# Pairs 0 and 1 projected among the seven value products, value weights summed in SBUF by accumulating DMAs, x mixed on VectorE

## The chip, the cores and the metric

The kernel runs on one core of one Trainium2 chip, in float32. The metric is device time in microseconds (us). TensorE (PE) multiplies; VectorE (DVE), ScalarE (ACT) and GpSimd (POOL) work on tiles; SP and POOL issue DMAs. A profile of one execution has the start and duration of each instruction, what released it, the DMA packets and the clock that TensorE was granted.

## What is computed

A trunk of two layers over 512 tokens of 1024 numbers: neighbourhood attention in layer 0, latent attention in layer 1, each with a SiLU gate, and a gated embedding behind each. The change is in layer 0, whose mixer is, cut short:

```python
def mixer_na(xn, w_in, rpb, w_out):
    q, k, v, z = jnp.split(xn @ w_in, 4, axis=-1)      # 1024 columns each, 16 heads of 64
    o = neighbourhood_attention(q, k, v, rpb)          # softmax over a window of keys
    return (o * jax.nn.silu(z)) @ w_out
```

`xn` is the input behind a root mean square norm. Queries, keys, gates and values are four products of `xn` with 1024 x 1024 weights.

## The kernel before, in words

**Split numbers.** A float32 operand is split into hi (rounded, a copy on ACT) and lo, the rest (operand minus hi, a subtraction on DVE or POOL). A product is hi·hi + lo·hi + hi·lo, three matmuls where there was one. So every weight piece of 128 x 1024 costs, ahead of its matmuls, a DMA into `wraw` (or `v`), an ACT copy (`whi`) and a DVE or POOL subtraction (`wlo`). Of `wraw`, `whi` and `wlo` there are three buffers each in the shared pool (`wp`).

**Gates first.** `run` (L1016) turns x into columns: `xT` holds normed x in two tiles of 4 x 512; copies `xh` (L1076, ACT) and rests `xl` (L1077, DVE and POOL in turn) are the right sides. In the meantime `z_phase` (L164) projects five gates (`z`), whose matmuls end the first part of TensorE's work.

**Values in seven products.** The value projection is a 2 x 2 block product computed with seven block products in place of eight (Strassen's scheme). The blocks are halves of x (tokens by halves of the 1024 numbers) and quarters of the weights. Products 7, 5, 6 and 3 need mixed x: four sums or differences of halves of `xT` on POOL (L1084), their copies `V7`, `V5`, `V6`, `V3` on ACT (L1087) and rests on DVE (L1088). Products 7, 6, 4 and 5 need mixed weights: `values_seven` (L224) loads four quarters in eight tiles `v` (L232), and DVE adds them in place (L246); copies (L251) are ACT's, rests (L253) DVE's and POOL's. The products go 1, 2, 7, 6, 4, 5, 3 (L283), 24 matmuls of 128 x 512 each, in six PSUM banks: 2 is summed into 1's banks, 4 into 7's, 5 and 3 into 6's. Between products DVE and ACT add and subtract banks (L268, L287 to L296) and split the results into the value tiles `Q` (L94, L96).

**Attention.** `na_heads` (L309) then runs over eight pairs of heads. `project(j)` (L314) loads the two weight pieces of the pair's queries and keys, multiplies them (two products of 24 matmuls, L107) and splits the results into `sa`, `sb` and `da`, `db` (halves by ACT copies), with rests on DVE. `attend(j)` (L347) runs the pair's two heads: scores (L404, L405), bias and row maxima on DVE, exponentials on ACT, the normalisation on POOL, transposes (L439, L441) and the product with the values (L453). The projections of pair j+1 go ahead of the attention of pair j. Between heads POOL issues DMAs (`sum_step`, L571) that sum the quarters of a later weight in DRAM; these are plain (bypass) or accumulating (add).

**What sets the order.** Each engine runs its own instructions in a fixed order, which a scheduler chose when the program was built; `issue_after` in the code ties one instruction behind another. A tile that reuses the memory of an older one waits for that one's readers.

Of the kernel before, what the change touches and what calls it, by code (L numbers as in the profile page):

```python
# [40 lines left out]
class Trunk:  # L41
# [182 lines left out]
    def values_seven(self, pool, xT, X, Q):  # L224

        nc = self.nc
        R = {p: [pool.tile([P, 1024], F32, name=f"v{p}{c}", bufs=1) for c in range(2)] for p in (1, 2, 3, 5)}
        src = {1: (0, 0), 2: (0, 2), 5: (1, 0), 3: (1, 2)}
        for p in (1, 2, 5, 3):
            for c in range(2):  # L230
                n, c0 = src[p]
                nc.sync.dma_start(R[p][c], self.a["na_v"][n, c0 + c])  # L232
        home = {7: (5, 5, 3, ALU.add), 6: (5, 5, 1, ALU.add), 4: (2, 2, 5, ALU.add), 5: (1, 5, 3, ALU.subtract)}
        order = (1, 2, 7, 6, 4, 5, 3)
        W, C, s1, s17, s6 = {}, {}, {}, {}, {}
        pieces = 0

        def prep(p):
            nonlocal pieces
            W[p] = []  # L240
            for c in range(2):
                raw = R[p][c] if p not in home else None
                if raw is None:
                    d, x, y, op = home[p]
                    raw = R[d][c]
                    nc.vector.tensor_tensor(out=raw, in0=R[x][c], in1=R[y][c], op=op)  # L246
                own = pieces < 5 or pieces % 5 < 3
                pieces += 1
                hi, lo = ((self.wp if own else pool).tile([P, 1024], F32R, name=t, tag=t if own else "vw", bufs=3 if own else 4)
                          for t in ("whi", "wlo"))  # L250
                nc.scalar.activation(hi, raw, AF.Copy)  # L251
                for o in (slice(0, S), slice(S, 2 * S)):
                    (nc.gpsimd if c else nc.vector).tensor_tensor(out=lo[:, o], in0=raw[:, o], in1=hi[:, o].bitcast(F32),  # L253
                                                                  op=ALU.subtract)
                W[p].append((hi, lo))

        def left(p, s, k, i):
            if p in X:
                return X[p][:, 2 * s + k // 2, k % 2 * 256 + i * P:k % 2 * 256 + (i + 1) * P]
            half, t = {1: (0, i), 2: (1, i), 4: (1, 2 + i)}[p]  # L260
            return xT[s][half][:, k, t * P:(t + 1) * P]

        def out(th, n, i, ps):
            self.v_split(Q[th, n][:, 2 * i:2 * i + 2, :], ps)

        banks = {1: "mm", 7: "S", 6: "T"}
        base = {2: 1, 4: 7, 5: 6, 3: 6}
        sub = lambda o, x, y: nc.vector.tensor_tensor(out=o, in0=x, in1=y, op=ALU.subtract)  # L268
        for p in order[:2]:
            prep(p)  # L270
        mm = self.last_mm
        for n, p in enumerate(order):
            if n + 2 < len(order):
                prep(order[n + 2])
            for i in range(2):
                if p in banks:
                    C[p, i] = self.psum(banks[p])
                ps = C[base.get(p, p), i]
                m = [(left(p, s, k, i), W[p][k // 2][r][:, k % 2 * S:(k % 2 + 1) * S])
                     for c in range(2) for s, r in ((0, 0), (1, 0), (0, 1)) for k in (2 * c, 2 * c + 1)]  # L280
                for j, (l, r) in enumerate(m):
                    with self.tc.issue_after(mm.ins):
                        mm = nc.tensor.matmul(ps, l, r, start=j == 0 and p in banks, stop=j == 11 and p in (2, 3, 4),  # L283
                                              skip_group_check=True)
                if p == 1:
                    s1[i] = self.temp("s1")
                    nc.scalar.activation(s1[i], ps, AF.Copy)  # L287
                elif p == 2:
                    out(0, 0, i, ps)
                elif p == 7:  # L290
                    nc.vector.tensor_tensor(out=ps, in0=ps, in1=s1[i], op=ALU.add)
                    s17[i] = pool.tile([P, S], F32, name="s17", tag="s", bufs=4)
                    nc.scalar.activation(s17[i], ps, AF.Copy)
                elif p == 6:
                    s6[i] = pool.tile([P, S], F32, name="s6", tag="s", bufs=4)
                    nc.scalar.activation(s6[i], ps, AF.Copy)  # L296
                    sub(C[7, i], C[7, i], s6[i])
                elif p == 4:
                    out(1, 0, i, ps)
                elif p == 5:  # L300
                    q = self.psum("O" if i else "T")
                    sub(q, ps, s17[i])
                    sub(ps, ps, s1[i])
                    out(1, 1, i, q)
                else:
                    out(0, 1, i, ps)
        self.last_mm = mm

    def na_heads(self, pool, xT, zs, oT, Q):  # L309
# [1019 lines left out]
```

## Time and profile before

| what | us |
|---|---|
| three runs | 674.4, 675.49, 675.76; median 675.49 |
| the profiled execution | 673.86 |
| its span, first to last instruction | 671.8 |
| PE busy | 644.6 |
| DVE, ACT, POOL busy | 436.5, 453.0, 448.4 |
| mean granted clock of PE | 0.983 |

A row of a group of instructions has line, engine, operation, out<-in by the program's names, shapes and the count, then the busy time. A row of a timeline starts with the start and duration in us; the time in brackets is the engine's idle time ahead of it and who ended it. A wait of PE costs time, since PE is busy 96% of the span; the others' waits cost only where PE waits for them.

### The profile page before, as it was taken

The numbers are of one execution on the slowest core, as the hardware profiler recorded it, in microseconds if no ns is written. First come the engines' busy times: TensorE is split into PE (matmuls) and PEld (weight loads), VectorE is DVE, ScalarE is ACT, GpSimd is POOL, SyncE is SP. The second block draws the span as 40 slices with busy tenths as digits, with TensorE's granted clock in tenths as the row PEclk, the third lists the DMA queues.
The fourth block names the chain that finished last, engine by engine and source line by source line (L and its number), as shares of the span: only waits on it lengthen the run. The fifth ranks groups of instructions, "written<-read, shape, count | busy, mean of one in ns | idle before, by whom it ended". The sixth has DMA issues, their size and how long they took to land.

```text
span 671.8 us, 9959 instructions
## 1 busy us (share of the span) xinstructions
PE 644.6 (96%) x3299; PEld 543.7 (81%) x3299; DVE 436.5 (65%) x880; ACT 453.0 (67%) x887; POOL 448.4 (67%) x393
## 2 busy tenths in 40 slices
PE   9965899999999999999999999999999999999994
PEld 6854678888888888888899888888888888888884
DVE  6278963557686752567861723688889886474675
ACT  7564454878787764388764544787988898536855
POOL 0496556659797865389844743685978978436974
PEclk9996999999999999999999999999999999999998
DMA  9880004549796999645644425320121213494524
GB/s 325 335 311 3 0 1 160 178 149 224 193 252 184 234 218 250 248 158 186 193 150 130 137 71 146 98 67 10 56 63 59 69 48 125 176 334 134 163 89 157
DMA packets 44755, 102.17 MB, mean 152 GB/s; under 512 B 4640, under 2 KB 17696, under 8 KB 44704
## 3 DMA queue, kind: packets, MB, share of 16 engines
q1 hardware_dynamic: 33776, 83.97, 37.1%
q0 software_dynamic: 10496, 16.78, 11.6%
q10 hardware_dynamic: 432, 0.79, 0.3%
q8 instruction: 26, 0.43, 0.3%
q14 instruction: 25, 0.20, 0.1%
HBM read 89.99 MB, written 25.17 MB: 171 GB/s over the span
## 4 chain that ended last, share of the span: by engine, by line
PE 90%; POOL 3%; DVE 2%; ACT 2%; issue 1%; DMA 1%; POOLq 0%; ACTq 0%; DVEq 0%
PE ps_mm L107 30%; PE ps_S L107 11%; PE ps_mm L804 6%; PE ps_T L139 6%; PE ps_T L696 5%; PE ps_O L916 4%; PE ps_mm L696 3%; PE ps_S L696 3%; PE ps_T L107 2%; PE ps_T L283 2%; PE ps_O L453 2%; PE ps_O L107 2%; PE ps_mm L754 2%; POOL xT L1084 2%; PE ps_mm L184 2%; PE ps_T L441 2%
## 5 line engine op out<-in xcount | busy, mean ns | idle before, releaser
L84 POOL TENSOR_TENSOR wwlo<-wraw,wwhi 128x1024 fp32r<-128x1024 f32 (+5 forms) x70 | 123.7, 1779 | 59.0 <-ACT wwhi L83 46.8
L641 POOL TENSOR_TENSOR wlo<-wraw,whi 128x512 fp32r<-128x512 f32 x56 | 72.6, 1335 | 23.3 <-ACT whi L639 21.2
L83 ACT ACTIVATE wwhi<-wraw 128x1024 fp32r<-128x1024 f32 (+5 forms) x73 | 57.2, 807 | 40.3 <-PE ps_mm L107 14.3
L901 POOL TENSOR_TENSOR ex<-ex,rc 128x512 f32<-128x512 f32 x64 | 66.1, 1041 | 26.5 <-DVE rc L900 22.4
L899 ACT ACTIVATE ex<-ps_S,mx 128x512 f32<-128x512 f32 x64 | 44.0, 687 | 12.1 <-DVE mx L897 10.5
L897 DVE TENSOR_REDUCE mx<-ps_S 128x1 f32<-128x512 f32 x64 | 43.7, 683 | 8.5 <-PE ps_S L107 7.6
L96 DVE TENSOR_TENSOR pt_lo<-ps_T,pt_hi 128x512 fp32r<-128x512 f32 x64 | 43.1, 681 | 7.1 <-ACT pt_hi L94 6.7
L427 POOL TENSOR_TENSOR ex<-ex,rc 128x128 f32<-128x128 f32 (+1 forms) x64 | 36.5, 640 | 14.3 <-DVE rc L423 13.5
L107 PE MATMUL ps_mm<-xh,wwhi 128*128 128x512 f32 x152 | 42.1, 403 | 0.0
L94 ACT ACTIVATE pt_hi<-ps_T 128x512 fp32r<-128x512 f32 x64 | 37.7, 595 | 3.3 <-PE ps_T L139 3.0
L107 PE MATMUL ps_mm<-xl,wwhi 128*128 128x512 f32 x152 | 40.0, 396 | 0.0
L107 PE MATMUL ps_mm<-xh,wwlo 128*128 128x512 f32 x152 | 39.3, 393 | 0.0
L139 PE MATMUL ps_T<-ident,ex 128*128 128x128 f32 x256 | 38.3, 272 | 0.0
L139 PEld LDWEIGHTS ps_T<-ident,ex 128*128 128x128 f32 x256 | 31.5, 140 | 7.5
L421 ACT ACTIVATE ex<-ex,mx 128x128 f32<-128x128 f32 (+1 forms) x64 | 30.3, 474 | 6.9 <-DVE mx L411 4.0
L253 POOL TENSOR_TENSOR wlo<-v,whi 128x512 fp32r<-128x512 f32 x14 | 22.7, 1647 | 17.6 <-ACT whi L251 17.5
L107 PEld LDWEIGHTS ps_mm<-xl,wwhi 128*128 128x128 f32 x152 | 28.0, 188 | 5.6
L107 PEld LDWEIGHTS ps_mm<-xh,wwlo 128*128 128x128 f32 x152 | 28.0, 188 | 5.6
L209 POOL TENSOR_TENSOR u<-u,z 128x512 f32<-128x512 f32 x16 | 21.5, 1345 | 16.2 <-DVE u L205 10.4
L639 ACT ACTIVATE whi<-wraw 128x1024 fp32r<-128x1024 f32 x28 | 29.3, 1057 | 3.4 <-DMA wraw<-sum 2.4
L107 PEld LDWEIGHTS ps_mm<-xh,wwhi 128*128 128x128 f32 x152 | 27.1, 189 | 4.6
L205 DVE TENSOR_TENSOR u<-ps_O,u 64x512 f32<-64x512 f32 x32 | 21.9, 684 | 12.7 <-ACT u L204 12.3
(465 smaller groups left out, 1936.6 us busy)
## 6 DMA issues: line engine op xcount, KB each, us to landing
sum<-gate POOLq DMA_DIRECT2D x12, 1024.0 KB, 8.2
wraw<-na_qk SPq DMA_DIRECT2D x16, 512.0 KB, 3.6
wraw<-sum SPq DMA_DIRECT2D x16, 512.0 KB, 3.3
pe<-pe SPq DMA_DIRECT2D x31, 256.0 KB, 6.3
wraw<-gate SPq DMA_DIRECT2D x12, 512.0 KB, 3.4
v<-na_v SPq DMA_DIRECT2D x8, 512.0 KB, 6.7
sum<-sum POOLq DMA_DIRECT2D x4, 1024.0 KB, 11.9
wraw<-na_o SPq DMA_DIRECT2D x8, 512.0 KB, 4.4
```

What stands on the lines that cost most here:

```text
L83: nc.scalar.activation(hi[:, c], raw[:, c], AF.Copy)
L84: f = lambda e, c=c: e.tensor_tensor(out=lo[:, c], in0=raw[:, c], in1=hi[:, c].bitcast(F32), op=ALU.subtract)
L94: self.last_copy = nc.scalar.activation(hi, src, AF.Copy, scale=scale)
L96: nc.vector.tensor_tensor(out=lo, in0=src, in1=hi.bitcast(F32), op=ALU.subtract)
L107: last = self.last_mm = nc.tensor.matmul(out, l, r, start=i == 0, stop=i == n - 1)
L139: self.last_mm = self.nc.tensor.transpose(t[:, i * P:(i + 1) * P], b, self.ident)
L641: nc.gpsimd.tensor_tensor(out=lo[:, o], in0=raw[:, o], in1=hi[:, o].bitcast(F32), op=ALU.subtract)
L696: mm = nc.tensor.matmul(ps, l, r, start=j == 0 and p in banks, stop=j == 11 and p in (2, 3, 4), skip_group_check=True)
L804: self.last_mm = nc.tensor.matmul(PS[key], *terms[i], start=i == 0, stop=i == len(terms) - 1)
L897: nc.vector.reduce_max(mx, sp, axis=AX.X, negate=True)
L899: nc.scalar.activation(ex, sp, AF.Exp, bias=mx, accum_out=sm)
L901: nc.gpsimd.tensor_tensor(out=ex, in0=ex, in1=rc.to_broadcast([P, S]), op=ALU.mult)
```

## The change

Three things move.

1. `na_heads` is entered before the values. Its `project` is cut into parts: `load(j)` (the weights), `product`, `queries` and `keys`. Pair 0 is projected ahead of value product 1, and pair 1 between products 2 and 7, through `early` (L338 is their matmul in the new numbering; L277 is that of the value products). Pair 0's weights and the first value piece are loaded and split while x is still being prepared. The attention's tiles `ex`, `pt` and so on are in a pool of their own (`nah`) that opens behind the values.
2. The value weights are no longer loaded as four quarters and added by DVE. Unmixed quarters are loaded piece by piece into `wraw`. The mixed ones come from two tiles of 1 MB: `T1` is loaded, and three accumulating DMAs, issued by POOL, add quarters to it one after another; its state after each is the weight of products 7, 6 and 4. `T2` is loaded and added to once (product 5). The rests of all value weights are DVE's. The banks of products 1 and 6 change (`S` and `mm` in place of `mm` and `T`).
3. The four mixes of x (L1137 now) are DVE's, no longer POOL's, and of the rests of x DVE makes the first four and POOL the last four, where they took turns.

```diff
+    def raw_piece(self, n, c, after=None):
+        raw = self.wp.tile([P, 1024], F32, name="wraw", tag="wraw", bufs=3)
+        with self.tc.issue_after(after.ins) if after else nullcontext():
+            self.nc.sync.dma_start(raw, self.a["na_v"][n, c])
+        return raw
+    def values_seven(self, pool, xT, X, Q, piece, project):
+        quarter = lambda n, c: self.a["na_v"][n, c:c + 2].rearrange("c p n -> p c n")
+        T = pool.tile([P, 2, 1024], F32, name="T1", bufs=1)
+        first = nc.sync.dma_start(T, quarter(1, 0))
+        T2 = pool.tile([P, 2, 1024], F32, name="T2", bufs=1)
+        add = lambda t, n, c: nc.gpsimd.dma_start(t, quarter(n, c), accum_op=ALU.add, max_dma_last_dim=4096)
+        add(T, 1, 2)
...
+        project(0)
+        W[1].append(made(self.raw_piece(0, 1, first), False))
+        W[2] = [made(self.raw_piece(0, 2 + c), True) for c in range(2)]
+        product(1)
+        project(1, True)
+        W[7] = [made(T[:, c, :], c) for c in range(2)]
+        product(2)
+        add(T, 0, 0)
+        project(1, False)
+        W[6] = [made(T[:, c, :], True) for c in range(2)]
+        product(7)
+        add(T, 0, 2)
+        nc.sync.dma_start(T2, quarter(1, 0))
+        add(T2, 0, 0)
+        W[4] = [made(T[:, c, :], False) for c in range(2)]
+        product(6)
+        W[5] = [made(T2[:, c, :], True) for c in range(2)]
+        product(4)
+        W[3] = [made(self.raw_piece(1, 2 + c), not c) for c in range(2)]
+        product(5)
+        product(3)
...
-                (nc.vector, nc.gpsimd)[k % 2].tensor_tensor(out=lo, in0=xs[k], in1=hi.bitcast(F32), op=ALU.subtract)
+                (nc.vector, nc.gpsimd)[k // 4].tensor_tensor(out=lo, in0=xs[k], in1=hi.bitcast(F32), op=ALU.subtract)
...
+            weights = {0: [self.load_w(a["na_qk"][i], 1024) for i in (0, 8)]}
+            piece = self.piece(None, self.raw_piece(0, 0), True)
...
-                nc.gpsimd.tensor_tensor(out=d, in0=d, in1=y, op=op)
+                nc.vector.tensor_tensor(out=d, in0=d, in1=y, op=op)
```

`made` is `piece`: an ACT copy and two half rests on DVE.

**The order on ACT.** Between the copies of mixed x (V) and those of the value weights (whi). Before, from the last gate on:

```order
L177 ACTIVATE z_487<-z_487 128x512
L1087 ACTIVATE V7_491<-xT_164 128x1024
L1087 ACTIVATE V5_495<-xT_164 128x1024
L1087 ACTIVATE V6_499<-xT_165 128x1024
L1087 ACTIVATE V3_503<-xT_165 128x1024
L251 ACTIVATE whi_533<-v10_517 128x1024
```

Now, over the same stretch (whi_504 is the first piece of product 1, whi_622 the second; sa to db are pair 0's queries and keys):

```order
L229 ACTIVATE whi_504<-wraw_502 128x1024
L177 ACTIVATE z_453<-z_453 128x512
L1140 ACTIVATE V7_510<-xT_164 128x1024
L177 ACTIVATE z_487<-z_487 128x512
L1140 ACTIVATE V5_514<-xT_164 128x1024
L1140 ACTIVATE V6_518<-xT_165 128x1024
L1140 ACTIVATE V3_522<-xT_165 128x1024
L344 ACTIVATE sa_577<-ps_mm_552 64x512
L345 ACTIVATE sb_578<-ps_mm_552 64x512
L362 ACTIVATE da_612<-ps_mm_587 64x512
...
L365 ACTIVATE db_613<-ps_mm_587 64x512
L229 ACTIVATE whi_622<-wraw_620 128x1024
```

The first value piece now stands ahead of all mixed x; the second stands behind the evacuation of pair 0's keys.

**The order on POOL.** From the gates' weights (wwlo_424, wwlo_458) to the values. Before:

```order
L84 TENSOR_TENSOR wwlo_424<-wraw_422,wwhi_423 128x1024
L84 TENSOR_TENSOR wwlo_458<-wraw_456,wwhi_457 128x1024
L1077 TENSOR_TENSOR xl0_156<-xT_164,xh0_154 128x512 x2
L1077 TENSOR_TENSOR xl1_157<-xT_165,xh1_155 128x512 x2
L1084 TENSOR_TENSOR xT_164<-xT_164 128x4x256
L1084 TENSOR_TENSOR xT_164<-xT_164,xT_165 128x4x256
L1084 TENSOR_TENSOR xT_165<-xT_165,xT_164 128x4x256
L1084 TENSOR_TENSOR xT_165<-xT_165 128x4x256
L253 TENSOR_TENSOR wlo_539<-v11_518,whi_538 128x512 x2
```

Now (wwlo_492 and wwlo_498 are pair 0's weights, wwlo_673 and wwlo_679 pair 1's; the DMAs are the adds):

```order
L84 TENSOR_TENSOR wwlo_424<-wraw_422,wwhi_423 128x1024
L84 TENSOR_TENSOR wwlo_458<-wraw_456,wwhi_457 128x1024
L84 TENSOR_TENSOR wwlo_492<-wraw_490,wwhi_491 128x1024
L1128 TENSOR_TENSOR xl1_157<-xT_165,xh1_155 128x512 x3
L84 TENSOR_TENSOR wwlo_498<-wraw_496,wwhi_497 128x1024
L1128 TENSOR_TENSOR xl1_157<-xT_165,xh1_155 128x512
...
L248 DMA T1_547<-na_v 128x2x1024
L248 DMA T2_550<-na_v 128x2x1024
L84 TENSOR_TENSOR wwlo_673<-wraw_671,wwhi_672 128x1024
L84 TENSOR_TENSOR wwlo_679<-wraw_677,wwhi_678 128x1024
L248 DMA T1_547<-na_v 128x2x1024 x2
L84 TENSOR_TENSOR wwlo_1125<-wraw_1123,wwhi_1124 128x1024
```

The mixes are gone; one rest of x stands behind wwlo_498; the second and third add to T1 stand behind pair 1's weights, with nothing between them.

**The order on TensorE.** From the last gate's product (ps_mm_462) on. Before, the value products come next:

```order
L107 MATMUL ps_mm_462<-rh0_150,wwlo_458 128x512 x4
L107 MATMUL ps_mm_462<-rh1_151,wwlo_458 128x512 x4
L283 MATMUL ps_mm_565<-whi_533,xh0_154 128x512 x2
L283 MATMUL ps_mm_565<-whi_533,xl0_156 128x512 x2
L283 MATMUL ps_mm_565<-wlo_534,xh0_154 128x512 x2
```

Now pair 0's queries (ps_mm_552) and keys (ps_mm_587) come first:

```order
L107 MATMUL ps_mm_462<-rh1_151,wwlo_458 128x512 x4
L338 MATMUL ps_mm_552<-xh0_154,wwhi_491 128x512 x4
L338 MATMUL ps_mm_552<-xh1_155,wwhi_491 128x512 x4
L338 MATMUL ps_mm_552<-xl0_156,wwhi_491 128x512 x4
L338 MATMUL ps_mm_552<-xl1_157,wwhi_491 128x512 x4
L338 MATMUL ps_mm_552<-xh0_154,wwlo_492 128x512 x4
...
L338 MATMUL ps_mm_587<-xh1_155,wwlo_498 128x512 x4
L277 MATMUL ps_S_641<-whi_504,xh0_154 128x512 x2
```

The 48 matmuls of pair 0 stand between the gates and the values; the last rest of x (xl1_157) is needed by the sixteenth of them.

More of the change, by code (lines that the diff above doesn't have):

```diff
@@ L221, in v_split, with piece @@
         self.split(hi, lo, src)
-    def values_seven(self, pool, xT, X, Q):
+    def piece(self, pool, raw, own):
         nc = self.nc
[L227 to L255, printed above, removed]
@@ new lines, in piece @@
+        hi, lo = ((self.wp if own else pool).tile([P, 1024], F32R, name=t, tag=t if own else "vw", bufs=3 if own else 4)
+                  for t in ("whi", "wlo"))
+        nc.scalar.activation(hi, raw, AF.Copy)
+        for o in (slice(0, S), slice(S, 2 * S)):
+            nc.vector.tensor_tensor(out=lo[:, o], in0=raw[:, o], in1=hi[:, o].bitcast(F32), op=ALU.subtract)
+        return hi, lo
+    def raw_piece(self, n, c, after=None):
[3 more added lines that the diff above has]
+        return raw
```

159 lines of the change are left out of this document (93 added, 66 removed).

## Prediction

> **What bounds the kernel now.** I read the page first, then the waits of TensorE, then its timeline and granted clock round the longest wait. The page:
>
> ```profile
> PE 644.6 (96%) x3299; PEld 543.7 (81%) x3299; DVE 436.5 (65%) x880; ACT 453.0 (67%) x887; POOL 448.4 (67%) x393
> PE   9965899999999999999999999999999999999994
> ```
>
> TensorE is the bound; one slice in 40 is 16.8 us, and the only holes ahead of the last slice are in slices 3 to 5. The waits of TensorE, longest first (who waits, for whom, total, times, longest):
>
> ```profile
> PE ps_mm L283 <- ACT whi L251: 13.5, 1, 13.5
> PE ps_T L283 <- POOL wlo L253: 1.9, 2, 1.7
> PE ps_S L283 <- DVE ps_S L268: 0.8, 2, 0.4
> PE ps_T L283 <- ACT whi L251: 0.6, 1, 0.6
> PE ps_S L283 <- POOL wlo L253: 0.5, 1, 0.5
> ```
>
> All are the value products: 17.3 us. TensorE's timeline gives the stretch to compare:
>
> ```profile
> 42.49 1.97 PE L107 MATMUL ps_mm<-rh,wwlo 128*128 128x512 f32 x8
> 57.98 1.22 PE L283 MATMUL ps_mm<-whi,xh 128*128 128x512 f32 x2 [13.51 <-ACT whi L251]
> 62.21 0.63 PE L283 MATMUL ps_mm<-wlo,xh 128*128 128x512 f32 x2
> 110.49 1.98 PE L107 MATMUL ps_mm<-xh,wwhi 128*128 128x512 f32 x8
> 115.93 1.98 PE L107 MATMUL ps_mm<-xh,wwhi 128*128 128x512 f32 x8
> 127.79 0.28 PE L404 MATMUL ps_S<-db,s 128*128 128x256 f32 x1
> ```
>
> From 110.49 to 115.93 are 24 matmuls: 0.227 us each. The gates' last matmul ends at 44.46. Up to 127.79 come seven products of 24, four projections of 24 (pairs 0 and 1) and the 8 short score matmuls of head 0: 264 x 0.227 + 1.0 = 60.9 us of work in 83.3 us. So 22.4 us are lost there. What the waits don't hold is mostly the clock:
>
> ```profile
> 60.00:62.00 2.00, 2.00 (x7) 1.55 (x6) 2.00 (x2) 0.00 (x0) 2.00 (x2) 0.51 0.00 0
> 62.00:64.00 2.00, 2.00 (x10) 1.59 (x9) 2.00 (x3) 0.75 (x2) 0.27 (x1) 1.00 0.00 0
> 84.00:86.00 2.00, 2.00 (x7) 1.56 (x6) 2.00 (x3) 1.53 (x3) 2.00 (x2) 0.54 0.00 0
> ```
>
> The columns after the busy times are granted clock, DMA share and GB/s. After the long gap the clock is half until 62: ten matmuls from 57.98 to 62.21 take 4.23 us where 2.27 would do, 2.0 us lost. Near 84 it happens again.
>
> Why the 13.5 us? ACT and POOL, in time:
>
> ```profile
> 35.92 4.27 ACT L1076 ACTIVATE xh<-xT 128x512 fp32r<-128x512 f32 x8
> ...
> 55.92 1.06 ACT L1087 ACTIVATE V<-xT 128x1024 fp32r<-128x1024 f32 x1 [2.22 <-POOL xT L1084]
> 56.88 2.94 ACT L251 ACTIVATE whi<-v 128x1024 fp32r<-128x1024 f32 x3
> ...
> 116.13 0.59 ACT L338 ACTIVATE da<-ps_mm 64x512 fp32r<-64x512 f32 x1 [0.70 <-PE ps_mm L107]
> ```
>
> ```profile
> 31.79 4.78 POOL L84 TENSOR_TENSOR wwlo<-wraw,wwhi 128x1024 fp32r<-128x1024 f32 x2 [4.40 <-PE ps_T L139]
> 37.13 7.47 POOL L1077 TENSOR_TENSOR xl<-xT,xh 128x512 fp32r<-128x512 f32 x4 [0.56 <-ACT xh L1076]
> 44.53 11.36 POOL L1084 TENSOR_TENSOR xT<-xT 128x1024 f32<-128x1024 f32 x4
> ```
>
> The row at 116.13 is used below. The weights' first copy (56.88) stands on ACT behind the last copy of mixed x, which waits for POOL's fourth mix (55.89). No transfer is waited for.
>
> **The change, part by part.** I follow the three waits it leaves; times are estimates on the axis of the old trace.
>
> *Pair 0 fills the hole.* Its 48 matmuls (10.9 us) start at 44.46 and don't need mixed x, and whi_504, the first value weights, is now copied ahead of it. So the wait on ACT goes. What is late next is the last rest of x. The durations, min/median/max in ns:
>
> ```profile
> L1077 POOL TENSOR_TENSOR xl<-xT,xh x4: 1297/1300/3705, 37.1 to 43.3; 128x512 fp32r<-128x512 f32 x4
> L1084 POOL TENSOR_TENSOR xT<-xT x4: 2348/2786/3202, 44.5 to 52.7; 128x1024 f32<-128x1024 f32 x4
> L1088 DVE TENSOR_TENSOR V<-xT,V x4: 1224/2811/3239, 48.0 to 57.0; 128x1024 fp32r<-128x1024 f32 x4
> ```
>
> ```profile
> 39.70 2.49 DVE L1077 TENSOR_TENSOR xl<-xT,xh 128x512 fp32r<-128x512 f32 x4
> ```
>
> ```profile
> L84 POOL TENSOR_TENSOR wwlo<-wraw,wwhi x8: 2380/2408/2412, 31.8 to 121.7; 128x1024 fp32r<-128x1024 f32 x8
> L251 ACT ACTIVATE whi<-v x14: 1040/1058/1062, 56.9 to 92.5; 128x1024 fp32r<-128x1024 f32 x14
> ```
>
> Beside each other DVE and POOL serve in turn: POOL's 3705 ns is its 1300 behind DVE's four, a DVE rest of 1224 takes up to 3239 beside POOL's mixes. POOL now makes rests 4 to 7 of x, with wwlo_498 (2.4) ahead of the last. It can't go on before about 42.2 (DVE's four end); then 4 x 1.3 + 2.4 = 7.6 us of its own, and between them two mixes (as long as a rest of 1024 numbers, 1.2) and two half rests of DVE (2.49 / 4 = 0.6), 3.6 together; that makes 53.4. TensorE asks for it at its 16th matmul, 44.46 + 15 x 0.227 = 47.9. **Term 1: 5.5 us** (0.6 if POOL is never held from 40.9 on, when ACT, with two more copies of 1.06 ahead, gives it the first part of x; 8 if DVE goes first each time). After such a gap the clock is half: **term 2: 2.0** (0 to 2).
>
> Then the key's evacuation: four half copies (0.59 each at 116.13) on ACT stand ahead of whi_622 (1.06), and the rest takes DVE 0.7 to 1.3; under it lie 12 matmuls (2.7). **Term 3: 1.3** (0 to 3). Products 1 and 2 so end at 44.46 + 96 x 0.227 + 8.8 = 75.1; call this E.
>
> *The sums in T1.* W7, W6 and W4 are one tile after one, two and three adds; each add waits until copy and rest of the one before have read it. The first is hidden under pair 0. POOL issues the second behind wwlo_679, at E + 6.2 (ACT: a bank copy of about 0.6 and wwhi_678, 1.06; POOL: 2.4; and DVE's rests of T1 in turn with it, some 2). An add takes L from issue to landing. The old kernel's first, third and fifth sums on POOL (plain, add, add of two sums):
>
> ```profile
> sum<-gate POOLq DMA_DIRECT2D x1, 1024.0 KB, 5.6
> ...
> sum<-gate POOLq DMA_DIRECT2D x1, 1024.0 KB, 9.2
> ...
> sum<-sum POOLq DMA_DIRECT2D x1, 1024.0 KB, 14.1
> ```
>
> ```profile
> q1 hardware_dynamic: 33776, 83.97, 37.1%
> q0 software_dynamic: 10496, 16.78, 11.6%
> ```
>
> Engine time per MB on q1 is 0.371 x 671.8 x 16 / 83.97 = 47.5 us. Half of q0's bytes are plain (398 us), which leaves 849 us for 8.39 MB of adds, 101 per MB: an add costs 2.1 times a plain transfer. Those adds go in pieces of 1 KB into DRAM; the new ones in 4 KB into SBUF, with idle DMA queues. I take L = 8.2, nearer to 9.2 because the second read stays; ends 5.6 and 14.1.
>
> On this the Trainium skill has a rule, DMA: Bandwidth & Descriptors, Anatomy of one DMA: about 2.0 us plus bytes over 436 GB/s, so 4.4 us for 1 MB. The trace's adds disagree (9.2); by the rule L would be 4.4 and term 5 nothing.
>
> The second add lands at E + 6.2 + L = E + 14.4; the copies and rests of its two pieces take 3.7 (1.06 and two rests of 1.3). TensorE has pair 1, the scores of head 0 and product 7 until E + 17.3, so product 6 waits hardly: **term 4: 0.5** (0 to 3). Without that wait it ends at E + 22.8. The third add is issued at E + 9.9 + L, and its first copy is ready at E + 11 + 2L. **Term 5: 2L - 11.8 - 0.5 = 4.1** (0 at L = 5.6; 15.9 at 14.1). Behind that waiting copy ACT holds whi_882, whi_840, whi_917 and s6_874; DVE subtracts s6_874 from bank T only behind four rests, and product 4's second half waits for it: **term 6: 3.0** (1 to 3.5). The gap may halve the clock: **term 7: 1.0** (0 to 2).
>
> *Edits at nothing.* DVE loses eight adds of weights and takes POOL's rests; outside terms 3 to 6 they lie under matmuls. T2's load and add have until product 5, some 30 us. The loads of pair 1 wait on SP behind T2 and the value pieces, but have 3.6 us to land in over 5:
>
> ```profile
> wraw<-na_qk SPq DMA_DIRECT2D x16, 512.0 KB, 3.6
> ```
>
> If T2 held SP 5 us longer, that would add up to 5.
>
> *Attention.* The softmax of head 0 now starts only after the last value bank, with pair 2's 10.9 us of matmuls over it. From then on the order is nearly the old one, and there
>
> ```profile
> 120.00:160.00 40.00, 40.00 (x220) 34.36 (x219) 25.06 (x81) 30.87 (x69) 28.32 (x28) 1.00 0.61 178
> ```
>
> TensorE was never idle while DVE, ACT and POOL had 15, 9 and 12 of 40 us free. They can catch up: **term 8: 1.0** (0 to 4).
>
> **Sum.** 5.5 + 2.0 + 1.3 + 0.5 + 4.1 + 3.0 + 1.0 + 1.0 = 18.4 us lost where 22.4 were: 4.0 us gained. All behind the stretch shifts with TensorE. The profiled execution took 673.86 (span 671.8): 669.9. It lies 1.6 under the median of 675.49, so the forecast for the median is 671.5.
>
> **Rivals.** *A: adds at the plain rate.* With L near 5.6 term 5 and 7 go and term 6 halves: 6.6 more, 10.6 gained, 664.9. For it: 4 KB pieces, idle queues; against: an add's second read. The rule above falls here.
>
> *B: slower, the chain of adds.* W6 and W4 can't overlap anything but their own product. At L = 11.5 product 6 waits 2, product 4 waits 23 - 11.8 - 2 = 9.2, the clock costs 2: 5.5 + 2 + 1.3 + 2 + 9.2 + 3 + 2 + 1 = 26.0, 3.6 lost, 679.1. It decides from about L = 10: each us counts twice, and by then the clock's second us has come. For it: the adds of 9.2 to 14.1; against: those shared the queues with weight loads.
>
> *C: gained, then given back.* Softmax trails the projections by a whole value stage, and some 4 us of waits appear in attention: no change, 675.5. Against: the free time above.
>
> **How the numbers follow.** Forecast 0.52, A 0.25, B 0.14, C 0.09. A change of 0.2%, 1.35 us, is about what the measurement can tell (the three runs span 1.36). Faster: forecast and A, 0.77; same: C, 0.09; slower: B, 0.14. The range reaches past A's 664.9 by 3 us for term 1 at its low end, and up to between C and B: 662 to 677.5.
>
> **What would show it.** Right: no wait on ACT near 44; a wait of L338 for POOL's xl near 48; a wait of product 4 (L277, ps_T) on ACT whi with the DMA of T1 behind it, and T1 adds of about 8 us. Term 1 is wrong if xl comes by 48, term 5 if the T1 adds land in under 6 us (A) or over 10 (B). The forecast is wrong altogether if the wait of product 1 remains, or if waits of several us appear behind 130 us.

## The result and the profile after

The changed kernel takes 669.94 us (median of 5 runs, 669.5 to 672.37) where the kernel before takes 675.49 in the same session: ratio 0.9929, 95% interval 0.9909 to 0.9949. It is faster by about 4.8 us. The profiled execution took 669.50 us with a span of 667.7, against 673.86 and 671.8.

The page after, its line of busy times and TensorE's 40 slices:

```profile
PE 646.0 (97%) x3299; PEld 543.5 (81%) x3299; DVE 429.7 (64%) x890; ACT 452.1 (68%) x887; POOL 422.2 (63%) x379
PE   9988987999999999999999999999999999999994
```

The deep hole in slice 4 (a 5) is gone, and shallower ones stand in slices 3, 4, 6 and 7. The waits of TensorE say what they are:

```profile
PE ps_T L277 <- ACT whi L229: 4.6, 1, 4.6
PE ps_mm L338 <- POOL xl L1128: 4.4, 1, 4.4
PE ps_mm L277 <- DVE lb L367: 1.7, 1, 1.7
```

The 13.5 us wait for the first value weights has gone; two of about 4.5 came, one of 1.7 and some under 1. TensorE's timeline places them (L338 is a projection among the products, L277 a value product, L455 head 0's scores, L107 at 123.83 the projection of pair 2):

```profile
42.31 1.98 PE L107 MATMUL ps_mm<-rh,wwlo 128*128 128x512 f32 x8
...
52.12 0.76 PE L338 MATMUL ps_mm<-xl,wwhi 128*128 128x512 f32 x1 [4.42 <-POOL xl L1128]
...
64.93 0.73 PE L277 MATMUL ps_S<-whi,xh 128*128 128x512 f32 x2 [0.73 <-ACT whi L229]
...
73.91 0.28 PE L455 MATMUL ps_S<-da,s 128*128 128x256 f32 x1
...
91.94 1.20 PE L277 MATMUL ps_mm<-whi,V 128*128 128x512 f32 x4 [0.56 <-ACT whi L229]
...
96.84 1.16 PE L277 MATMUL ps_mm<-whi,V 128*128 128x512 f32 x4 [1.68 <-DVE lb L367]
...
99.23 0.61 PE L277 MATMUL ps_mm<-wlo,V 128*128 128x512 f32 x2
104.42 1.22 PE L277 MATMUL ps_T<-whi,xh 128*128 128x512 f32 x2 [4.57 <-ACT whi L229]
...
109.97 0.83 PE L277 MATMUL ps_T<-whi,xh 128*128 128x512 f32 x2
...
112.94 1.07 PE L277 MATMUL ps_mm<-whi,V 128*128 128x512 f32 x4
...
123.83 1.98 PE L107 MATMUL ps_mm<-xh,wwhi 128*128 128x512 f32 x8
```

The same 60.9 us of work now lie between 44.29 (the end of the row at 42.31) and 123.83: 79.5 us, where the kernel before took 83.3. So 18.6 us are lost instead of 22.4. What comes behind is unchanged: 667.7 - 123.83 = 543.9 us, before 671.8 - 127.79 = 544.0.

The clock granted behind the two long waits (the column after the five engines' busy times):

```profile
52.00:54.00 2.00, 1.88 (x5) 1.51 (x6) 2.00 (x2) 0.03 (x1) 1.79 (x5) 0.55 0.88 352
54.00:56.00 2.00, 2.00 (x7) 1.60 (x6) 2.00 (x3) 1.06 (x1) 1.74 (x2) 0.60 0.04 10
...
106.00:108.00 2.00, 2.00 (x6) 1.52 (x5) 2.00 (x4) 1.69 (x3) 0.00 (x0) 0.50 0.00 0
```

The clock is half from the wait at 104.42 up to 110. POOL makes the late rest of x and issues the adds into T1, at 54.31, 81.60 and 94.97 (the add left out, at 67.06, goes into T2):

```profile
49.82 2.25 POOL L1128 TENSOR_TENSOR xl<-xT,xh 128x512 fp32r<-128x512 f32 x1
...
54.31 1.43 POOL L248 DMA_DIRECT2D T<-na_v  x1
...
81.60 1.19 POOL L248 DMA_DIRECT2D T<-na_v  x1 [1.69 <-issue]
94.97 1.20 POOL L248 DMA_DIRECT2D T<-na_v  x1 [12.18 <-DVE wlo L231]
```

ACT takes up the second sum at 90.83 (the row stands with the experiment on the keys' copies), 9.2 us behind its add's issue.

### The profile page after: what moved, and what is told of

Its sections match the earlier page's. It is cut to its first block, busy times and chain, and to the rows that moved or that the text cites. A ratio compares the mean times of both kernels' runs of the same rounds, so it can differ in the third digit from the quotient of the medians.

```text
span 667.7 us, 9952 instructions
## 1 busy us (share of the span) xinstructions
PE 646.0 (97%) x3299; PEld 543.5 (81%) x3299; DVE 429.7 (64%) x890; ACT 452.1 (68%) x887; POOL 422.2 (63%) x379
## 4 chain that ended last, share of the span: by engine, by line
PE 83%; DMA 8%; ACT 2%; DVE 2%; issue 2%; POOL 2%; POOLq 0%; SPq 0%; DVEq 0%; ACTq 0%
PE ps_mm L107 27%; PE ps_S L107 10%; PE ps_mm L855 7%; PE ps_T L139 6%; PE ps_T L747 5%; PE ps_O L967 4%; PE ps_mm L747 3%; PE ps_S L747 3%; DMA T<-na_v 3%; PE ps_O L504 2%; PE ps_T L107 2%; PE ps_O L107 2%; DMA wraw<-na_z 2%; PE ps_mm L805 2%; PE ps_mm L277 2%
## 5 line engine op out<-in xcount | busy, mean ns | idle before, releaser
L83 ACT ACTIVATE wwhi<-wraw 128x1024 fp32r<-128x1024 f32 (+5 forms) x73 | 57.1, 805 | 30.6 <-PE ps_mm L107 13.5
L107 PE MATMUL ps_mm<-xh,wwhi 128*128 128x512 f32 x120 | 32.5, 400 | 0.0
L107 PE MATMUL ps_mm<-xh,wwlo 128*128 128x512 f32 x120 | 32.2, 396 | 0.0
L107 PE MATMUL ps_mm<-xl,wwhi 128*128 128x512 f32 x120 | 32.1, 397 | 0.0
L209 POOL TENSOR_TENSOR u<-u,z 128x512 f32<-128x512 f32 x16 | 22.0, 1372 | 14.4 <-DVE u L205 10.4
L107 PE MATMUL ps_S<-ko,qo 128*128 128x512 f32 x96 | 28.9, 409 | 0.0
L107 PE MATMUL ps_S<-ke,qe 96*128 96x512 f32 x96 | 28.6, 406 | 0.0
L855 PE MATMUL ps_mm<-cT,wwhi 128*128 128x512 f32 x94 | 27.7, 393 | 0.0
L204 ACT ACTIVATE u<-ps_O 64x512 f32<-64x512 f32 x32 | 19.0, 593 | 12.4 <-PE ps_O L504 9.1
```

The source lines that it names most:

```text
L83: nc.scalar.activation(hi[:, c], raw[:, c], AF.Copy)
L107: last = self.last_mm = nc.tensor.matmul(out, l, r, start=i == 0, stop=i == n - 1)
L855: self.last_mm = nc.tensor.matmul(PS[key], *terms[i], start=i == 0, stop=i == len(terms) - 1)
```

## The experiments

My theory: the pairs' projections fill the hole, and what is left is first an instruction out of place on POOL, then a chain of adds of 8 to 9 us each that nothing but one product can cover. The rivals: that it is the move of the mixes to VectorE which gains; that relieving VectorE by DMA adds is what gains; and that the adds cost nothing that is seen. All kernels are the changed kernel with one edit unless said otherwise. Each ratio is against the kernel before in the same session. A span is that of the one profiled execution; other executions of a kernel lie up to 3.4 us from it, so where ratios and spans differ, the ratios decide.

| Kernel | ratio to the kernel before | 95% interval | span |
|---|---|---|---|
| changed kernel | 0.9929 | 0.9909 to 0.9949 | 667.7 |
| one part: mixes on VectorE, in the kernel before | 0.9944 | 0.9923 to 0.9964 | 668.2 |
| one part: pairs among the products | 0.9869 | 0.9849 to 0.9889 | 665.6 |
| two parts: pairs and mixes, sums on VectorE | 0.9845 | 0.9823 to 0.9867 | 662.3 |
| two parts: pairs and DMA sums, mixes on POOL | 0.9994 | 0.9983 to 1.0005 | 673.0 |
| pair 1 behind the products | 1.0037 | 1.0022 to 1.0053 | 677.3 |
| plain DMAs (sums left out) | 0.9786 | 0.9770 to 0.9803 | 659.9 |
| third sum on VectorE | 0.9884 | 0.9867 to 0.9901 | 665.9 |
| rests of x first | 0.9873 | 0.9858 to 0.9889 | 666.2 |
| both of these | 0.9846 | 0.9831 to 0.9862 | 663.6 |
| pair 1's keys first | 0.9915 | 0.9898 to 0.9932 | 668.2 |
| rests first, all sums on VectorE | 0.9793 | 0.9774 to 0.9813 | 660.1 |
| that, and two copies on POOL | 0.9818 | 0.9797 to 0.9839 | 661.2 |

**Which part gains.** The mixes alone, in the kernel before:

```diff
-                nc.gpsimd.tensor_tensor(out=d, in0=d, in1=y, op=op)
+                nc.vector.tensor_tensor(out=d, in0=d, in1=y, op=op)
```

> The kernel before with one part of the change: the four mixes of x on VectorE instead of GpSimd. No pair is projected early, and no DMA adds into SBUF. My theory (the hole of 13.5 us is ACT's copies of mixed x ahead of the weights; with VectorE mixing, the mixes end near 48 and the weights' copy near 51): the wait falls from 13.5 to 6 or 7 us, the half clock behind it stays, and the kernel gains 5 to 7 us: 668.5 to 670.5, about as much as the whole change gave, so that the rest of the change moves losses more than it removes them. Rival (pair 0 in the hole is what matters; VectorE is slowed by POOL's rests beside it and mixes no faster): the wait stays above 10 us and the kernel within 3 us of 675.5.

Measured 671.33 us, 3.8 us faster than before by its ratio. TensorE's wait for the value weights:

```profile
53.67 1.22 PE L283 MATMUL ps_mm<-whi,xh 128*128 128x512 f32 x2 [9.17 <-ACT whi L251]
```

ACT ahead of it:

```profile
51.61 1.06 ACT L1087 ACTIVATE V<-xT 128x1024 fp32r<-128x1024 f32 x1 [1.54 <-DVE xT L1084]
52.58 2.94 ACT L251 ACTIVATE whi<-v 128x1024 fp32r<-128x1024 f32 x3
```

The copy of the weights (52.58) still stands behind the last copy of mixed x, now for VectorE's mixes, which alternate with its own rests of V. The wait fell by 4.3 us, not by 7, and the 5 to 7 us that I gave this part were too much. Another wait, of 3.7 us on VectorE's subtraction between products (L268), where 0.4 was the longest before, came up ahead of product 4: two rests of the weights, 3.0 us long beside POOL's rests, stand ahead of it on VectorE. The rival, a wait above 10 us, fell narrowly (9.2). By its total alone this part could pass for the whole change (0.9944 and 0.9929); the next runs show that it isn't.

The pairs alone are the two edits of the next two experiments put together (mixes on POOL, sums on VectorE):

> Of the three parts of the change only one: pairs 0 and 1 among the products, but the mixes of x on GpSimd and the sums on VectorE as in the kernel before. My theory (pair 0 fills the hole whoever mixes; with the mixes on GpSimd pair 0's evacuation on ACT waits some 3 us longer behind the copies of mixed x, and that is all): 3 to 5 us slower than with the mixes on VectorE, 667.5 to 669.5, faster than before by 6 to 8. Rival (the move of the mixes is what gains, the pairs alone nothing): within 2 us of the kernel before.

Measured 667.09, 8.8 us faster than before by its ratio, a little more than the 6 to 8 I expected. The rival, that the pairs alone gain nothing, falls. This part takes in all that is left of the change: the value weights loaded piece by piece, the other banks, the early first value piece, all weight rests on VectorE and the new division of the rests of x. No run tests these without the pairs.

The sums made by VectorE, all else as in the changed kernel:

```diff
-        add = lambda t, n, c: nc.gpsimd.dma_start(t, quarter(n, c), accum_op=ALU.add, max_dma_last_dim=4096)
+        def add(t, n, c):
+            for i in range(2):
+                nc.vector.tensor_tensor(out=t[:, i, :], in0=t[:, i, :], in1=self.raw_piece(n, c + i), op=ALU.add)
```

> The changed kernel with all four accumulating DMAs undone: each sum is made by two additions on VectorE from the value pieces in SBUF, as in the old kernel's weights. My theory (the adds in T1 are a serial chain of about 9 us each, and VectorE has time to spare): product 4's wait goes and product 6's does too; VectorE gets eight more additions of 1.2 to 2.5 us, which lie under matmuls: 4 to 7 us faster than the changed kernel, 663 to 666. Rival (the accumulating DMAs are what brings the gain, since they take the sums off a VectorE that is held up by POOL): VectorE becomes late for the rests of the weights, products wait on DVE 5 us or more in sum, and the kernel is as slow as before or slower, 674 to 678.

Measured 664.72, inside the 663 to 666 of my theory. Its two longest waits of TensorE:

```profile
PE ps_mm L341 <- POOL xl L1131: 4.4, 1, 4.4
PE ps_S L280 <- DVE wlo L231: 2.3, 1, 2.3
```

Products 6 and 4 are in no row any more. VectorE is late once, by 2.3 us, where two additions stand ahead of rests. So relieving VectorE by DMA adds is worth at most this wait, and on balance it costs: by the ratios the accumulating DMAs lose 0.0084 of 675.5, 5.7 us (5.4 in the spans).

The mixes put back on GpSimd, DMA sums kept:

```diff
-                nc.vector.tensor_tensor(out=d, in0=d, in1=y, op=op)
+                nc.gpsimd.tensor_tensor(out=d, in0=d, in1=y, op=op)
```

> The changed kernel with the four mixes of x back on GpSimd, all else as changed. My theory (pair 0 fills the hole that the mixes made, so where they run matters little to the first products; but POOL issues the adds, and 8 to 11 us of mixes stand ahead of the first one): the 13.5 us wait does not come back, the first add goes out near 63 instead of 54.3, and the second and third slip by 2 to 5 us: 2 to 5 us slower than the changed kernel, 672 to 675. Rival (mixing on VectorE is what took the wait away): a wait of 8 us or more for mixed x is back ahead of the first products and the kernel is at 676 or above.

Measured 674.83, the same as the kernel before (0.9994, 0.9983 to 1.0005), 4.4 us slower than the changed kernel by the ratios. No wait of 13.5 came back, but this one, inside product 1:

```profile
67.64 1.22 PE L277 MATMUL ps_S<-whi,xh 128*128 128x512 f32 x2 [4.87 <-ACT whi L229]
```

POOL there, the four mixes and the first add:

```profile
50.54 11.50 POOL L1137 TENSOR_TENSOR xT<-xT 128x1024 f32<-128x1024 f32 x4
...
64.28 1.43 POOL L248 DMA_DIRECT2D T<-na_v  x1
```

The mixes hold the issue of the first add until 64.28 (54.31 in the changed kernel), and ACT's evacuation of pair 0, at 63.04, stands behind the last copy of mixed x. The second and third add go out at 87.47 and 100.77, 5.9 and 5.8 us later than in the changed kernel. What the mixes' place is worth seems to depend on who adds: 1.6 us by the ratios with sums on VectorE (0.9869 against 0.9845, intervals that overlap; 3.3 in the spans, and 3 to 5 were expected), 4.4 with adds that POOL issues (5.3 in the spans); the intervals are too wide to show that these two differ. The theory's range of times held, at its upper end, though the adds slipped by more than its 2 to 5 us. The rival named a wait of 8 us or more that did not come; its conclusion, that without the moved mixes nothing is gained, holds with DMA adds and not without them (8.8 us).

**What hides the adds.** Pair 1 projected behind the last product (its two project(1, ...) lines out of the sequence, one project(1) at its end):

```diff
-        project(1, True)
...
-        project(1, False)
...
         product(3)
+        project(1)
```

> The changed kernel with the projections of pair 1 made behind the last value product instead of among the products; the sums still by accumulating DMAs. My theory (10.9 us of matmuls of pair 1 are what hides the second add): product 6 is asked for 10.9 us earlier, its add still lands near 90, so TensorE waits about 9 to 10 us there and 4 to 5 again ahead of product 4, with the half clock behind each: 9 to 11 us slower than the changed kernel, 679 to 681. Rival (pair 0 in the hole is the whole gain, pair 1 only moves): within 2 us of 669.9.

Measured 677.76 us, 7.3 us slower than the changed kernel by the ratios and 9.6 in the spans, slower than the kernel before. But I had the place half wrong. Two of its waits of TensorE:

```profile
PE ps_mm L277 <- ACT whi L229: 5.1, 1, 5.1
...
PE ps_O L503 <- DVE pl L96: 2.5, 1, 2.5
```

The second add's issue on POOL:

```profile
76.79 1.19 POOL L248 DMA_DIRECT2D T<-na_v  x1 [9.67 <-issue]
```

Product 6 waits 5.1 us, not 9 to 10, because the second add goes out at 76.79 instead of 81.60. It waits for the last rest of product 7's weights on VectorE, which ends at 76.26 instead of 81.06: ACT no longer has the copies of pair 1's weights between the two copies for product 7, and VectorE's rests no longer take turns with POOL's rests of pair 1's weights (74.08 and 77.50 in the changed kernel). The end of pair 1's projection, with which the same work is done as in the changed kernel at 123.83:

```profile
127.09 1.98 PE L337 MATMUL ps_mm<-xh,wwlo 128*128 128x512 f32 x8
```

It ends at 129.07: 5.2 us of the 9.6. The other 4.4 are lost behind it, in attention, where the wait of 2.5 us on VectorE's pl appears; from 160 to 180 TensorE is busy for 17.5 of 20 us and the clock is 0.91. The profiled execution is one of the longer ones (679.11 us, of 675.67 to 679.67), so the share of attention may be less in others.

That is the third rival of the prediction (given back in attention). It can happen; with pair 1 among the products it doesn't.

**What an add costs.** The four DMAs without their accumulation:

```diff
-        add = lambda t, n, c: nc.gpsimd.dma_start(t, quarter(n, c), accum_op=ALU.add, max_dma_last_dim=4096)
+        add = lambda t, n, c: nc.gpsimd.dma_start(t, quarter(n, c), max_dma_last_dim=4096)
```

> The changed kernel with the four adding DMAs made plain: they overwrite T1 and T2, so the sums of the weights are left out of the computation, and the time shows only what accumulating costs. My theory (an add reads its destination too, and so takes longer than a plain transfer): the transfers land in about 5.5 us instead of 8.3 to 9.2, the third one is hidden under product 6, product 4's wait of 4.57 goes: 4 to 7 us faster than the changed kernel, 663 to 666. Rival (the 8 to 9 us are queueing and issue on POOL's queue, not the accumulation): landing stays over 7.5 us, and the time within 2 us of 669.9.

Measured 661.69, 9.7 us faster than the changed kernel by the ratios, more than I expected. The transfers into T1 and T2, with the median time from issue to landing, and their queue's packets, MB and share of the 16 engines' span, in the changed kernel:

```profile
T<-na_v POOLq DMA_DIRECT2D x4, 1024.0 KB, 8.9
...
q0 software_dynamic: 11584, 20.97, 15.5%
```

The same without accumulation:

```profile
T<-na_v POOLq DMA_DIRECT2D x4, 1024.0 KB, 5.3
...
q0 software_dynamic: 11584, 20.97, 13.7%
```

Accumulating costs 3.6 us of 8.9 by the medians (8.3 to 9.2 in T1 and 13.0 in T2, against 5.2 to 5.4). The queue's engine time says the same: 16 x (0.155 x 667.7 - 0.137 x 659.9) = 209 us for four adds, 52 for one, 3.3 us on each of 16 engines. The Trainium skill (DMA: Bandwidth & Descriptors, Anatomy of one DMA) has a rule by which a transfer of 1 MB takes an estimated 4.4 us; the plain ones here took 5.3, so the rule comes within 1 us of them; the adds take twice what it gives. With plain transfers both waits of the chain are gone: the prediction's first rival, adds at the plain rate, would have been right in its mechanism (with 9.7 us more gained, not 6.6), and falls by its condition.

**The two waits one at a time.** The third sum alone on VectorE:

```diff
-        add(T, 0, 2)
+        for c in range(2):
+            nc.vector.tensor_tensor(out=T[:, c, :], in0=T[:, c, :], in1=self.raw_piece(0, 2 + c), op=ALU.add)
```

> The changed kernel with the third sum in T1 made by two additions on VectorE out of the value pieces in SBUF, the other adds left to DMAs. My theory (the third add can't overlap anything but product 6, so its 8.3 us are seen): product 4's wait of 4.57 us goes, so does the half clock behind it (1 to 2 us), and product 6 is no worse: 5 to 7 us faster than the changed kernel, about 664. Rival (VectorE's relief is what the accumulating DMAs bring; two additions of 1.2 to 3 us on it between the rests cost as much as the DMA did): product 4 waits on DVE instead, 3 us or more, and the time is within 2 us of 669.9.

Measured 668.13 us, 3.0 us faster than the changed kernel by the ratios (1.8 in the spans), half of what I expected. TensorE's waits behind the first products (the 4.4 us on xl and two of under 1 us elsewhere are left out):

```profile
PE ps_mm L277 <- DVE lb L368: 3.7, 1, 3.7
PE ps_mm L277 <- ACT whi L229: 1.0, 1, 1.0
...
PE ps_T L277 <- DVE ps_T L261: 0.4, 1, 0.4
```

Product 4's wait fell to 0.4, but product 6's second bank now waits 3.7 instead of 1.7: on VectorE the two additions stand ahead of the rests of pair 1's keys (lb), whose bank that product needs. The rival had the right mechanism for half of the sum.

The last rest of x ahead of wwlo_498 on POOL:

```diff
-            weights = {0: [self.load_w(a["na_qk"][i], 1024) for i in (0, 8)]}
+            weights = {0: [self.load_w(a["na_qk"][0], 1024)]}
+            with tc.issue_after(rest.ins):
+                weights[0].append(self.load_w(a["na_qk"][8], 1024))
```

> The changed kernel with GpSimd's rest of the weights wwlo_498 (2.79 us) put behind the last rest of x instead of ahead of it. My theory (the wait of 4.4 us near 48 is one instruction out of place on POOL): the last xl ends near 49.5 instead of 52.07, the wait of TensorE on it falls from 4.4 to about 1.5 or less, and of the eight matmuls at half clock behind it (1.4 us too long) little is left; pair 0 and products 1 and 2 end 3 to 4.5 us earlier, and with them everything behind, if the adds follow: about 666 us. Rival (the sums in T1 set the time whatever comes ahead): the second add still goes out near 81.6, TensorE waits at product 6 for what it gained, and the kernel stays near 669.9. Second rival: wwlo_498 itself is now late, the key's projection waits 2 us or more, and half of the gain is lost.

Measured 667.83, 3.8 us faster than the changed kernel by the ratios (1.4 to 6.1 between the ends of their intervals), 1.5 in the spans. On TensorE the wait fell as expected, and another came up behind it:

```profile
48.86 0.50 PE L338 MATMUL ps_mm<-xl,wwhi 128*128 128x512 f32 x1 [1.13 <-POOL xl L1128]
...
62.30 0.74 PE L277 MATMUL ps_S<-whi,xh 128*128 128x512 f32 x2 [2.95 <-ACT whi L229]
```

ACT ahead of the second one:

```profile
56.74 1.06 ACT L1142 ACTIVATE V<-xT 128x1024 fp32r<-128x1024 f32 x1 [1.21 <-DVE xT L1139]
...
61.20 2.94 ACT L229 ACTIVATE whi<-wraw 128x1024 fp32r<-128x1024 f32 x3
```

Pair 0 is done earlier, but its evacuation and the weights' copy behind it (61.20) stand on ACT behind the last copy of mixed x, whose mix VectorE ends no sooner than before. So the old kernel's hole is still there, covered by pair 0: whoever shortens the cover meets it. My second rival had the half gain right and its cause wrong; wwlo_498 was in time.

Both edits together:

> Both of the other two edits in one kernel: the last rest of x ahead of wwlo_498, and the third sum in T1 on VectorE. My theory: the two waits lie in a row on TensorE, so the gains add up as far as the second add can follow: 8 to 10 us faster than the changed kernel, 660 to 662. Rival (the second add, issued behind wwlo_679 and landing 9 us later, is next): product 6 then waits 2 to 4 us, and the sum of the two gains is not reached: 663 to 665.

Measured 665.63, ratio 0.9846: 5.6 us faster than the changed kernel by the ratios, far from the 8 to 10 of the theory and just above the rival's 663 to 665. The two gains as measured (3.0 and 3.8) would add up to 6.8. The two new waits just shown (3.7 and 3.0) are in it: the rival's wait at product 6 came, but on VectorE's rests of the keys and not on the second add.

**Is a wait a loss?** Pair 1's key copies ahead of the copies of T1's second sum on ACT (the copies of W6 tied behind the last key copy):

```diff
-            nc.scalar.activation(db[0:64], psk[64:128], AF.Copy)
+            self.last_key = nc.scalar.activation(db[0:64], psk[64:128], AF.Copy)
...
-        W[6] = [made(T[:, c, :], True) for c in range(2)]
+        with self.tc.issue_after(self.last_key.ins):
+            W[6] = [made(T[:, c, :], True) for c in range(2)]
```

> The changed kernel with pair 1's key copies put ahead of the copies of T1's second sum on ACT, where they no longer wait for its add. My theory (product 4 is held by the chain of adds, whose third goes out when the rests of the second sum are made, wherever the keys' copies stand): the wait of 1.68 us at product 6 goes, product 4's wait grows from 4.57 to about 6.2, and the time is within 1 us of 669.9. Rival (each wait on TensorE is a loss by itself): 1.7 to 2.5 us faster, about 668.

Measured 669.95, ratio 0.9915 against 0.9929, with intervals that overlap, and 0.5 us longer in the span: no difference that can be told. ACT at that place in the changed kernel, where the copies da and db stand behind the wait for the add:

```profile
90.83 2.01 ACT L229 ACTIVATE whi<-T 128x1024 fp32r<-128x1024 f32 x2 [9.09 <-DMA T<-na_v]
92.86 0.59 ACT L362 ACTIVATE da<-ps_mm 64x512 fp32r<-64x512 f32 x1
```

And here:

```profile
87.97 0.59 ACT L366 ACTIVATE db<-ps_mm 64x512 fp32r<-64x512 f32 x1
91.86 2.01 ACT L229 ACTIVATE whi<-T 128x1024 fp32r<-128x1024 f32 x2 [3.30 <-DMA T<-na_v]
```

The longest wait of TensorE here:

```profile
PE ps_T L277 <- ACT whi L229: 6.5, 1, 6.5
```

The intervals alone would leave room for the rival; the trace decides against it. The wait of 1.7 on lb is gone and product 4's grew from 4.6 to 6.5, so product 4 starts no sooner (105.43 against 104.42). Up to product 4 the chain of adds sets the time, and waits ahead of it only share out what it takes.

**Both causes removed.** The rests first, and all sums on VectorE:

> The two edits that gained most, in one kernel: all sums of the weights made on VectorE instead of by DMAs, and the last rest of x ahead of wwlo_498. My theory: the first edit ended the waits behind 85 us (span 662.3 us), the second takes 1.6 us or more off what comes before 74, and nothing behind it now depends on a chain of transfers that would eat it: 660 to 661.5 us of span, a time near 663. Rival (pair 0's copies stand on ACT behind the copies of mixed x, so that what the rest of x gains the value weights lose): within 1 us of the version with the sums on VectorE alone, 664.7.

Measured 661.99 us, ratio 0.9793 (0.9774 to 0.9813): the fastest of all that leave nothing out, and 9 us faster than the changed kernel by the ratios. What is left ahead of and inside the first product is the wait on ACT of the edit with the rests of x first (2.9 us), one of 1.4 on DVE's rests, and the half clock behind them, which lasts from 62.6 to about 72: 18 matmuls take 8.2 us where 4.1 would do. The last kernel tried to take the first away by having POOL copy two of the mixed x:

```diff
-                nc.scalar.activation(h, d, AF.Copy)
+                if p in (7, 5):
+                    nc.scalar.activation(h, d, AF.Copy)
+                else:
+                    nc.gpsimd.tensor_copy(h, d)
```

> The kernel of the other entry with both edits, and the copies of the last two mixed x made by GpSimd instead of ACT. My theory (the wait of 2.95 us for the second block of product 1's weights, which came up when the rest of x was moved, is ACT holding pair 0's evacuation behind a copy that waits for VectorE's last mix): that wait falls below 1 us, and the kernel gains another 1 to 2 us, about 661.5. Rival (POOL and VectorE serve in turn, so two more copies on POOL slow the mixes and the rests of V on VectorE by as much): no gain, within 0.7 us of the other entry, or a new wait on DVE.

Measured 663.44 us, no gain (0.9818). Its longest wait of TensorE:

```profile
PE ps_S L280 <- DVE wlo L231: 5.8, 1, 5.8
```

ACT's wait fell to 0.7 as expected, and VectorE's took its place: its last mix and rest wait for POOL, and the sums and rests of the weights follow 1.1 us later than without the edit. The rival was right. In that stretch VectorE is the next limit.

## Why the prediction was right, and where it was not

The forecast was a gain of 4.0 us from 22.4 lost to 18.4. Measured were 18.6 in the stage. The two longest waits came where they were forecast, but that the net agrees so well is luck: errors of 2.7 us and less, up and down, cancel. By its steps:

| Step | predicted | measured | from |
|---|---|---|---|
| 1 to 3: up to the end of products 1 and 2 | 8.8 | 7.8 | 44.29 to 73.91, less 96 x 0.227 |
| of it the last rest of x | 5.5 | 4.4 | row at 52.12 |
| of it the key's evacuation | 1.3 | 0.7 | row at 64.93 |
| 4: product 6 | 0.5 | 3.2 | 73.91 to 99.84, less 17.3 and 5.45 |
| 5: third add | 4.1 | 4.6 | row at 104.42 |
| 6 and 7: product 4 and its clock | 4.0 | 3.1, all of it beside the half clock | 104.42 to 112.94, less 5.45 |
| 8: attention | 1.0 | 0.0 | 543.9 against 544.0 behind the stage |
| sum (18.6 before rounding the steps) | 18.4 | 18.7 | |

- *The hole.* Pair 0 in it was right, and the pairs alone show 8.8 us. The forecast gave the mixes' move no term of its own; with DMA adds it is worth 4.4 by the ratios, and mixes on POOL put off the first add's issue by 10 us.
- *Term 1* was right in cause and 1.1 too large: POOL's last rest ended at 52.07, not 53.4. Putting it first took the wait to 1.1. What the forecast did not see is that this wait covered another (ACT behind VectorE's last mix), so that it is not worth 4.4 to remove.
- *Term 2* fits: 52 to 56 at 0.55 and 0.60 of the clock loses 1.7 of the 2.0.
- *Term 4* is the step that was mis-sized, 0.5 against 3.2. The forecast listed what stands on ACT behind the copies that wait for an add only for the third add, and not for the second, where pair 1's four key copies stand and product 6's second bank needs them. Of these 2.7, the 1.7 of that wait are no loss of their own: without it product 4 started no sooner. The list alone would have cost nothing, though, had the second add landed at E + 14.4 as forecast, which is 88.3 (E, the end of products 1 and 2, is 73.91 here). By an estimate from the rows, from 90.83, when the copies began, to the end of lb at 96.70 are 5.9 us, and 88.3 + 5.9 = 94.2 lies ahead of 95.16, when TensorE was ready for the second bank (with plain DMAs the transfer landed by 86.25 and this wait is not there). The add landed at E + 16.9, the other half of this step.
- *Term 5* came out at 4.6 by partly wrong numbers: the second add went out 7.7 us behind E, not 6.2, and landed in 9.2 instead of 8.2; the delays at product 6 hid part of that. Why it went out late stands in ACT's row of the copy ahead of wwlo_679:

```profile
76.37 1.06 ACT L83 ACTIVATE wwhi<-wraw 128x1024 fp32r<-128x1024 f32 x1 [1.66 <-DMA wraw<-na_qk]
```

The load of pair 1's second weights took 8.3 us to land, beside the add into T2, where the forecast gave it 3.6 and counted it among the edits at nothing. With plain DMAs ACT did not wait there, and the second transfer went out 0.8 us earlier (80.78).
- *Terms 6 and 7* came out at 3.1 of 4.0 together, but they don't add up as the forecast had it. TensorE had no wait between the halves of product 4: the first half's twelve matmuls take from 104.42 to 109.97, 5.55 us where 2.72 would do, for the clock is half. The subtraction that term 6 is about ends just ahead of the second half, at 109.91:

```profile
109.22 0.69 DVE L261 TENSOR_TENSOR ps_T<-ps_T,s 128x512 f32<-128x512 f32 x1
```

So the half clock covers the wait. By these rows TensorE at full clock would have been done at 107.14 and would have waited some 2.8 us for the subtraction (an estimate). With plain DMAs, where no gap halves the clock, such a wait shows: 1.3 us on L261.
- *Term 8* was too careful: nothing was given back. It needs pair 1 late to be seen.

The rival of adds at the plain rate fell by 3.6 us an add. The slower rival needed adds of 10 us; those in T1 took 8.3 to 9.2. Its margin was thin: with the mixes on POOL and the first add out 10 us later, nothing of the gain is left. Left open is why the add into T2 took longest, 13.0 us: it ran beside loads on SP's queue, but no kernel was run without these.

## What to carry to other kernels

Split a change into its parts before crediting it: here moved projections gave 8.8 us and the accumulating DMAs took 5.7 back, which the total of 4.8 does not show. Sums that follow one another in one tile are a chain whose links are each a whole transfer, an issue and a copy; hide them or keep them on an engine with free time. And a wait on the bounding engine is a loss only if nothing late stands right behind it: look for what would be asked for next before you price its removal.

## What the runs showed of the hardware

- An accumulating DMA of 1 MB into SBUF took 8.9 us from issue to landing where the same transfer without accumulation took 5.3, in pieces of the same size, and its issue on POOL took 1.21 us instead of 0.75 (min/median/max in ns). With accumulation:

```profile
L248 POOL DMA_DIRECT2D T<-na_v x4: 1194/1210/1431, 54.3 to 95.0; - x4
```

and without:

```profile
L248 POOL DMA_DIRECT2D T<-na_v x4: 716/746/975, 54.4 to 90.4; - x4
```

- VectorE and POOL held each other for whole instructions in these two rows. With the rests first, the rest of V on VectorE:

```profile
49.81 3.43 DVE L1143 TENSOR_TENSOR V<-xT,V 128x1024 fp32r<-128x1024 f32 x1
```

and the rest of the weights on POOL:

```profile
48.77 3.39 POOL L84 TENSOR_TENSOR wwlo<-wraw,wwhi 128x1024 fp32r<-128x1024 f32 x1
```

VectorE's 3.43 us are the wait until POOL ends at 52.16 (2.35) and some 1.1, where such an instruction alone takes 1.2. The Trainium skill (SBUF — State Buffer, SBUF: two separate sides) states this as an exclusive lock on the port pair that the two share, held by whichever starts first; these rows agree.

- The clock was halved behind every gap of TensorE of 2.3 us and more in the value stage of all these kernels, for 3 us at the least, and for over 9 us where another gap of 1.4 followed soon (62.6 to 72 with the rests first and all sums on VectorE). One gap of 1.68 us (96.84 in the changed kernel) left it at 1.00; one of 1.71 at 82.80 in the kernel before, just behind two short ones, was followed by 0.54. The gap of 1.13 us at 48.86, with the rests first, left it at 1.00; the one of 2.95 at 62.30 did not (windows of that kernel):

```profile
48.00:50.00 2.00, 1.14 (x5) 0.97 (x6) 2.00 (x2) 0.08 (x1) 2.00 (x2) 1.00 0.63 221
...
64.00:66.00 2.00, 2.00 (x6) 1.53 (x6) 2.00 (x5) 0.74 (x2) 0.00 (x0) 0.50 0.90 320
```
